# Four adaLN gate chunks of the second layer moved into its attention, and RMS and LayerNorm roots as one GpSimd power

## The chip, the cores and the metric

The kernel runs on one core of one Trainium2 chip. The metric is the device time of one execution in microseconds (us). TensorE (PE), VectorE (DVE), ScalarE (ACT), GpSimd (POOL) and SyncE (SP) work beside one another, each with its own queue of instructions; SP and POOL also issue DMAs from theirs.

## The reference, cut to what matters

Two layers work on 640 tokens (128 of context, 512 latent, D = 1024). The gate that the change moves is the last third of `mod`; the roots that it rewrites are those of `rms_norm(x, norm_g)` and of the convolution's `layer_norm`.

```
def trunk_layer(x, cond, p, latent, k_ctx, v_ctx):
    mod = silu(cond) @ p['w_ada'] + p['b_ada']        # 1024 x 3072
    shift, scale, gate = split(mod, 3, axis=-1)
    h = rms_norm(x, p['norm_g']) * (1.0 + scale) + shift
    y, k, v = parallel_mixer(h, p, latent, k_ctx, v_ctx)
    return x + gate * y, k, v

def rms_norm(x, g):   y = x * rsqrt(mean(x * x, -1) + EPS);  return y * g
def layer_norm(x, g, b):
    xc = x - mean(x, -1)
    return xc * rsqrt(mean(xc * xc, -1) + EPS) * g + b
```

`parallel_mixer` projects h by `w_in` (1024 x 11264) and runs four branches on it: a convolution module with that LayerNorm, a Hyena long convolution, a pooling mixer, and attention. Their gated outputs go through `wo_*`, are merged, and go through `w_out`. The gate is used only where the layer's output is added to x, so the second layer's gate is needed at its very end.

## The kernel before, in words

Every large matrix product is done in three products of halves: a weight tile of 512 KB is split into `whi` and `wlo`, the activations into a high and a low part (both called `sl` in the trace). `weights()` takes one of three pairs of whi/wlo buffers (the ring `wr`), SP loads the tile into one of two `raw` buffers, ACT casts it to `whi` and writes minus `whi` into `wlo`, and POOL issues a DMA that adds the tile to `wlo` in place (line 347). PE then multiplies 16 instructions with `whi` and 8 with `wlo` for each half of 320 tokens.

The adaLN product is cut into twelve chunks of 256 columns for each layer. `ada_chunk(l, j)` takes one slot of the same ring `wr`, but without a cast: SP loads the two halves of a chunk straight into the `whi` and `wlo` buffer (line 658), PE multiplies eight instructions of 32x256, which the trace shows as 16 records (`ax<-whi,cs` and `ax<-wlo,cs`, eight of each), and ACT copies the result to a tile `k`. Chunks 8 to 11 are the gate: SP stores `k` to DRAM as `grow` (line 672), and `gate_rows(l)` reads it back near the layer's end. `ada_later(jobs, step, start)` runs a list of chunks as a background thread: it waits `start` us of the planner's clock, and `step` us behind each chunk.

The order of work is made by a planner in Python, the class `Loom`: each stage is a thread with a priority (a smaller number goes first), and the planner, with its own modelled clocks, writes PE's order by hand. The other engines take their instructions in an order that follows from it, and SP and POOL issue their DMAs in that order. So a thread that is spawned elsewhere also changes the planner's later choices.

The first layer's four gate chunks and eight of the second layer's chunks run as a thread of priority 5 in the first layer's attention, one every `ASTEP` = 14 us. The second layer's four gate chunks run between the layers: they are spawned when the first layer's `out_proj` begins, with start `GS` = 40 us, no step and priority 50. At the same place `modulated(1, ...)` makes the second layer's h, in two groups of 128-token tiles (three, then two): `rms()` sums the squares and takes the root on DVE (`rmsv`, then `rmsr`), PE transposes it to a row (`ax<-ident,rmsr`), ACT copies the row (`t<-ax`), and for each of eight k DVE multiplies (`u<-sl,t`) and ACT and DVE write the two halves of h (`sl<-u,mod` and `sl<-u,mod,sl`). Behind it PE begins the second layer's `w_in`.

`rsqrt()` makes a root of 11 small DVE instructions: a first guess by two integer operations, and three Newton steps of three. `power()` is one `tensor_tensor` of POOL with the operation pow; before the change only the Hyena filters use it (`frs<-fv,nhalf`). `Conv.norm` takes the LayerNorm's root in each layer (`lnv`, then `lnr`), and PE spreads it by transposes (`sc<-ident,lnr`).

Of the kernel before, what the change touches and what calls it, by code (L numbers as in the profile page):

```python
# [21 lines left out]
DEPTH = 2  # L22
# [12 lines left out]
HW = 80  # L35
HA = 40
PL = 1
GS = 40.0
EACH = 0.003
ORD = "01456237vkq"  # L40
WAHEAD = 120
# [6 lines left out]
ASTEP = 14.0  # L48
ASTART = 60.0
LATA = 1.2  # L50
# [182 lines left out]
def hybrid_flow_backbone(ctx: ExitStack, tc: tile.TileContext, i, o):  # L233
    nc = tc.nc
    lm = Loom()
# [23 lines left out]
    def nm(p):  # L259
        count[0] += 1  # L260
        return f"{p}{count[0]}"
# [52 lines left out]
    def split(hi, lo, src, scale=None):  # L314
        if scale is None:
            act.copy(hi, src)
            dve.tensor_tensor(out=lo, in0=src, in1=r32(hi), op=ALU.subtract)
        else:
            act.activation(out=hi, in_=src, func=AF.Copy, scale=scale)
            dve.scalar_tensor_tensor(out=lo, in0=src, scalar=scale, in1=r32(hi),  # L320
                                     op0=ALU.mult, op1=ALU.subtract)
# [59 lines left out]
    def new_act(n):  # L381
        hi = yield from slots(n, F32R)
        lo = yield from slots(n, F32R)
        return Act(hi, lo)
# [102 lines left out]
    def power(out, v, n):  # L487

        pool.tensor_tensor(out=out, in0=v, in1=nhalf.to_broadcast([P, n]), op=ALU.pow)

    def rsqrt(out, v, n):

        t = sm.tile([P, 40], F32, tag="rsq_t", name=nm("rt"))[:, 0:n]
        dve.tensor_scalar(out=out.bitcast(I32), in0=v.bitcast(I32), scalar1=1, scalar2=None,
                          op0=ALU.logical_shift_right)
        dve.tensor_scalar(out=out.bitcast(I32), in0=out.bitcast(I32), scalar1=-1.0,
                          scalar2=1597463007.0, op0=ALU.mult, op1=ALU.add)
        for _ in range(3):
            dve.tensor_tensor(out=t, in0=out, in1=out, op=ALU.mult)
            dve.scalar_tensor_tensor(out=t, in0=t, scalar=-0.5, in1=v, op0=ALU.mult, op1=ALU.mult)  # L500
            dve.scalar_tensor_tensor(out=out, in0=t, scalar=1.5, in1=out, op0=ALU.add, op1=ALU.mult)
# [38 lines left out]
    def par(l, ct, row):  # L540
        return prm[:, ct, pcol(l, row):pcol(l, row) + 1]
# [150 lines left out]
    def ada_finish(l, p):  # L692

        ng = prm[:, 2 * (p % 2):2 * (p % 2) + 2, pcol(l, R_NG) + p // 2]
        for cnd in range(2):
            v = mods[l][:, 1, 2 * p:2 * p + 2, cnd]
            dve.scalar_tensor_tensor(out=v, in0=v, scalar=1.0, in1=ng, op0=ALU.add, op1=ALU.mult)
        ev_mod[l][p].set()
# [10 lines left out]
    def ada_later(jobs, step, start):  # L709
        yield lm.pe + start  # L710
        for l, j in jobs:
            yield from ada_chunk(l, j)
            if 4 <= j < 8:
                ada_finish(l, j - 4)
            yield lm.pe + step
# [34 lines left out]
    def rms(ssq):  # L750
        n = ssq.shape[1]
        v = sm.tile([P, 5], F32, tag="rmsv", name=nm("rmsv"))[:, 0:n]
        rs = sm.tile([P, 5], F32, tag="rmsr", name=nm("rmsr"))[:, 0:n]
        dve.tensor_reduce(out=v, in_=ssq, axis=AX.X, op=ALU.add)
        dve.tensor_scalar(out=v, in0=v, scalar1=1.0 / D, scalar2=EPS, op0=ALU.mult, op1=ALU.add)
        rsqrt(rs, v, n)
        return rs

    def modulated_first(a, xs, ssq):
# [89 lines left out]
    def merge(l, b, ga, nk, wo, merged, mode, ma=None, wait=None):  # L849


        for d in range(8):
            if mode == "last" and d % 4 == 0:
                for part in (ma.hi, ma.lo):
                    part.append((yield from slot(F32R)))
            th = yield from tr.get(T)

            def gate(j, ps):
                act.activation(out=th[:, 320 * j:320 * j + 320], in_=ps, func=AF.Tanh, scale=0.5)

            yield from in_proj(l, C_GM + b * D + 128 * d, gate)
            if wait is not None:
                yield wait
            w = yield from weights(wo[:, 128 * d:128 * d + 128].rearrange("(k p) c -> p k c", p=P), nk, 128)
            def take(j, ps):
                tj = th[:, 320 * j:320 * j + 320]
                dve.scalar_tensor_tensor(out=tj, in0=tj, scalar=1.0, in1=ps, op0=ALU.add, op1=ALU.mult)

            yield from both(w, 0, ga, nk, take)
            wr.put(WD)  # L870
            if mode == "first":
                sp.dma_start(out=mscr[l, d], in_=th)
                lm.cur.t += 2.5
            else:
                yield lambda: 0.0 if len(merged) == 2 else INF
                mv = merged[d // 4].v((d % 4) * T, T)
                dve.tensor_tensor(out=mv, in0=mv, in1=th, op=ALU.add)
                if mode == "last":
                    split(ma.h(d), ma.l(d), mv, 0.5)
            tr.put()  # L880
# [735 lines left out]
    class Conv:  # L1616
# [58 lines left out]
        def norm(self):  # L1675

            l = self.l
            yield self.ev_tap
            co = self.co
            pm = yield from sc.get()  # L1680
            for j in range(2):
                pe.matmul(pm[:, j, 0:328], lnw.to_broadcast([P, P]), self.pad.v(328 * j, 328), start=True, stop=True)
            self.pad.free()
            for c in range(4):
                x = co.v(656 * c, 656)
                xh = x.rearrange("p (a b) -> p a b", a=2)
                yield turn
                dve.tensor_tensor(out=xh, in0=xh, in1=pm[:, :, 0:328], op=ALU.subtract)
            sc.put()
            for c in range(4):  # L1690
                sq = yield from ur.get(656)
                act.activation(out=sq, in_=co.v(656 * c, 656), func=AF.Square)
                if c == 0:
                    total = sq
                else:
                    dve.tensor_tensor(out=total, in0=total, in1=sq, op=ALU.add)
                    ur.put()
            yield lm.sync()
            pvv = yield from ax.get()
            for t in range(5):  # L1700
                t0 = 0 if t == 0 else 143 + 128 * (t - 1)
                pe.matmul(pvv[:, t:t + 1], total[:, t0:t0 + 128], lnw, start=True, stop=True)
            ur.put(0.0)
            v = sm.tile([P, 5], F32, tag="lnv", name=nm("lnv"))
            rs = sm.tile([P, 5], F32, tag="lnr", name=nm("lnr"))
            dve.tensor_scalar(out=v, in0=pvv[:, 0:5], scalar1=EPS, scalar2=None, op0=ALU.add)
            ax.put()
            rsqrt(rs, v, 5)
            yield lm.sync()
            pr = yield from sc.get()  # L1710
            for t in range(5):
                dst = pr[:, 1, 0:128] if t == 0 else pr[:, 0, 128 * (t - 1):128 * t]
                pe.transpose(dst, rs[:, t:t + 1].to_broadcast([P, P]), ident)
            self.sa = sa = yield from new_act(1)
            for c in range(4):
                x = co.v(656 * c, 656)
                xn = yield from ur.get(T)
                dve.tensor_tensor(out=xn[:, 0:128], in0=x[:, 0:128], in1=pr[:, 1, 0:128], op=ALU.mult)
                yield turn
                dve.tensor_tensor(out=xn[:, 128:640], in0=x[:, 143:655], in1=pr[:, 0, :], op=ALU.mult)  # L1720
                yield turn
                dve.tensor_scalar(out=xn, in0=xn, scalar1=par(l, c, R_LNG), scalar2=par(l, c, R_LNB),
                                  op0=ALU.mult, op1=ALU.add)
                th = yield from ur.get(T)
                act.activation(out=th, in_=xn, func=AF.Tanh, scale=0.5)
                yield turn
                dve.scalar_tensor_tensor(out=xn, in0=th, scalar=1.0, in1=xn, op0=ALU.add, op1=ALU.mult)
                ur.put()
                split(sa.h(c), sa.l(c), xn, 0.5)
                ur.put()  # L1730
            sc.put()
            co.free()
            self.ev_norm.set()
# [157 lines left out]
    def layers():  # L1891
# [3 lines left out]
        for l in range(DEPTH):  # L1895
# [37 lines left out]
            lm.spawn(at.values_out(), 0, LATV)  # L1933
            lm.spawn(at.run(), 5.5)
            lm.spawn(at.parts(), 4)
            yield hy.ev_done
            yield from merge(l, 1, hy.gb, 4, i["wo_hyena"][l], None, "first")
            hy.gb.free()
# [35 lines left out]
            else:  # L1974
                load_x(xs, scratch[0:LP], scratch[LP:T])
            ssq = sm.tile([P, 5, 4], F32, tag="ssq", name=nm("ssq"))
            if l + 1 < DEPTH:
                lm.spawn(ada_later([(1, j) for j in range(8, 12)], 0.0, GS), 50, LATA)
            if l + 1 < DEPTH:
                xT = yield from slots(2)  # L1980
                evs = [[Event(lm) for _ in range(2)] for _ in range(4)]
# [180 lines left out]
```

## Time and profile before

| | |
|---|---|
| three runs, us | 2267.57, 2272.85, 2273.87 (median 2272.85) |
| the profiled execution, us | 2271.39 |
| its span, us | 2269.6 |
| granted TensorE clock, mean of the span | 0.992 |
| PE busy | 2189.7 us (96%), 15951 instructions |
| DVE, ACT, POOL busy | 59%, 52%, 26% |

The span is what lies between the first and the last instruction of the trace; the time of the execution is 1.8 us more. A row of a timeline gives start and length in us, then the engine, the line, the operation, the names (written from read), the size of one, and how many follow one another; in brackets stands how long the engine was idle just before, and what it waited for. Windows give busy time of each engine in a stretch, and the granted clock as a share of full speed.

### The profile page before, as it was taken

The page shows a single profiled execution, that of the slowest core. Times are in us where ns is not written, and L with a number is a line of the kernel's source. Part 1 is how long each engine was busy: PE and PEld are TensorE (multiplying, and loading weights), DVE is VectorE, ACT ScalarE, POOL GpSimd, SP SyncE. Part 2 cuts the span into 40 slices and gives each one's busy share as a digit, 9 for nine tenths or more (in the row PEclk, how much of TensorE's full clock was granted, in tenths as well). Part 3 has the DMA queues.
Part 4 walks back from the last instruction along what each step waited for, and adds up shares of the span by engine and source line. Part 5 has one row for each costly group of instructions (what it writes and reads, how often), then busy time and mean ns, then how long its engine had stood idle before and what let it go on. Part 6 is the DMA issues. An engine that isn't in the chain of part 4 may idle for free. (4 is left out here: it accounts for less than half of the span.)

```text
span 2269.6 us, 40007 instructions
## 1 busy us (share of the span) xinstructions
PE 2189.7 (96%) x15951; PEld 2140.5 (94%) x15951; DVE 1329.2 (59%) x2791; ACT 1190.8 (52%) x2179; POOL 585.5 (26%) x451
## 2 busy tenths in 40 slices
PE   5999999999999999999997999999999999999999
PEld 3899999999999998999996999999999999999999
DVE  5676786656679945443224677855764899612222
ACT  5544457667664345444445544656676543544442
POOL 1744321111012222554211333111111122222221
PEclk9899999999999999999998999999999999999999
DMA  8476775545568879778898865555466698698986
GB/s 277 110 156 137 156 159 114 97 95 99 106 122 147 149 126 182 154 164 161 150 220 239 154 118 120 110 102 101 84 110 118 126 155 150 120 162 148 174 171 138
DMA packets 510536, 322.33 MB, mean 142 GB/s; under 512 B 13016, under 2 KB 499608, under 8 KB 510093
## 3 DMA queue, kind: packets, MB, share of 16 engines
q0 software_dynamic: 223856, 122.96, 42.7%
q1 hardware_dynamic: 285780, 196.68, 28.6%
q8 instruction: 125, 2.05, 0.4%
q14 instruction: 62, 0.51, 0.1%
q10 hardware_dynamic: 713, 0.14, 0.0%
HBM read 302.26 MB, written 17.47 MB: 141 GB/s over the span
## 5 line engine op out<-in xcount | busy, mean ns | idle before, releaser
L193 PE MATMUL mm<-sl,whi 128*128 128x320 f32 x6304 | 1059.1, 313 | 10.6 <-DVE t L178 3.2
L193 PEld LDWEIGHTS mm<-sl,whi 128*128 128x128 f32 x6304 | 951.2, 189 | 18.2 <-DVE sl L178 4.3
L193 PE MATMUL mm<-sl,wlo 128*128 128x320 f32 x3152 | 555.1, 312 | 5.7 <-DMA wlo<-in_w_in_dram 5.7
L347 POOL DMA_DIRECT2D wlo<-in_w_in_dram x173 | 264.4, 1532 | 915.6 <-ACT wlo L178 689.5
L193 PEld LDWEIGHTS mm<-sl,wlo 128*128 128x128 f32 x3152 | 484.0, 189 | 7.4 <-DMA wlo<-in_w_in_dram 6.7
L178 ACT CAST whi<-raw 128x1024 fp32r<-128x1024 f32 (+2 forms) x272 | 255.3, 939 | 429.4 <-PE mm L193 405.1
L178 ACT ACTIVATE wlo<-whi 128x1024 fp32r<-128x1024 f32 (+2 forms) x269 | 254.9, 948 | 29.6 <-PE mm L193 25.7
L178 DVE SCALAR_TENSOR_TENSOR t<-t,mm 128x320 f32<-128x320 f32 x192 | 93.0, 485 | 294.1 <-PE mm L193 244.4
L193 PE MATMUL mm<-whi,sl 128*128 128x256 f32 x1600 | 226.2, 284 | 2.5 <-ACT u L178 1.5
L178 DVE SCALAR_TENSOR_TENSOR sc<-sl,prm,sc 128x640 f32<-128x640 f32 (+14 forms) x232 | 207.3, 893 | 11.4 <-ACT sc L178 6.7
L193 PE MATMUL sc<-sl,sl 128*128 128x128 f32 (+1 forms) x1344 | 203.4, 293 | 5.7 <-DVE u L178 2.8
L193 PEld LDWEIGHTS mm<-whi,sl 128*128 128x128 f32 x1600 | 203.3, 188 | 4.8 <-ACT u L178 1.7
L178 DVE TENSOR_TENSOR h<-ax,h 128x512 fp32r<-128x512 f32 (+1 forms) x200 | 120.1, 604 | 118.7 <-ACT h L178 117.5
L193 PEld LDWEIGHTS sc<-sl,sl 128*128 128x128 f32 x1344 | 179.5, 194 | 8.0 <-DVE u L178 4.0
L178 ACT ACTIVATE t<-mm 128x320 f32<-128x320 f32 x208 | 90.0, 433 | 137.8 <-PE mm L193 135.1
L178 DVE TENSOR_SCALAR_CACHE_REDUCE u<-sc,rq 128x640 f32<-128x640 f32 x128 | 112.6, 880 | 46.2 <-PE sc L193 45.2
L178 ACT ACTIVATE u<-u,nb 128x640 f32<-128x640 f32 x128 | 106.2, 830 | 52.3 <-DVE u L178 51.6
L178 ACT CAST h<-ax 128x512 fp32r<-128x512 f32 (+1 forms) x200 | 102.5, 515 | 55.8 <-PE ax L202 53.6
L193 PE MATMUL mm<-wlo,sl 128*128 128x256 f32 x800 | 126.7, 281 | 4.4 <-DMA wlo<-in_w_in_dram 4.4
L193 PE MATMUL ax<-h,sl 128*128 128x256 f32 (+1 forms) x656 | 120.7, 295 | 4.0 <-DVE h L178 2.7
L202 PE MATMUL ax<-ident,u 128*128 128x128 f32 x752 | 118.5, 273 | 4.7 <-DVE h L178 2.6
L193 PEld LDWEIGHTS mm<-wlo,sl 128*128 128x128 f32 x800 | 108.3, 188 | 5.0 <-DMA wlo<-in_w_in_dram 5.0
(211 smaller groups left out, 2225.9 us busy)
## 6 DMA issues: line engine op xcount, KB each, us to landing
raw<-in_w_in_dram SPq DMA_DIRECT2D x176, 512.0 KB
wlo<-in_w_in_dram POOLq DMA_DIRECT2D x173, 512.0 KB, 6.6
wlo<-in_w_ada_dram SPq DMA_DIRECT2D x19, 512.0 KB
whi<-in_w_ada_dram SPq DMA_DIRECT2D x19, 512.0 KB
raw<-in_wo_attn_dram SPq DMA_DIRECT2D x16, 512.0 KB
wlo<-in_wo_attn_dram POOLq DMA_DIRECT2D x16, 512.0 KB, 6.4
raw<-in_w_out_dram SPq DMA_DIRECT2D x16, 512.0 KB
wlo<-in_w_out_dram POOLq DMA_DIRECT2D x16, 512.0 KB, 6.0
```

The source lines that it names most:

```text
L178: r = f(*args, **kw)
L193: r = self.real.matmul(out, lhsT, rhs, **kw)
L202: r = self.real.transpose(out, in_, ident)
L347: nc.gpsimd.dma_start(out=lo[:, 0:w].rearrange("p (k c) -> p k c", k=kk), in_=src.bitcast(F32R), accum_op=ALU.add)
```

## The change

Two things change. The four gate chunks of the second layer are no longer spawned between the layers but behind the second layer's `at.parts()`, with step 14 us and priority 5. And `rms()` (three calls: 128x5 at the start, 128x3 and 128x2 between the layers) and `Conv.norm` (128x5 in each layer) call `power()` instead of `rsqrt()`. The roots of the attention's head norms stay on DVE.

```
@@ -35,7 +35,6 @@
-GS = 40.0
@@ -753,7 +752,7 @@            (rms)
         dve.tensor_scalar(out=v, in0=v, scalar1=1.0 / D, scalar2=EPS, op0=ALU.mult, op1=ALU.add)
-        rsqrt(rs, v, n)
+        power(rs, v, n)
         return rs
@@ -1705,7 +1704,7 @@          (Conv.norm)
             ax.put()
-            rsqrt(rs, v, 5)
+            power(rs, v, 5)
             yield lm.sync()
@@ -1933,6 +1932,8 @@          (the layers' main thread)
             lm.spawn(at.parts(), 4)
+            if l:
+                lm.spawn(ada_later([(1, j) for j in range(8, 12)], ASTEP, 0.0), 5, LATA)
             yield hy.ev_done
@@ -1974,8 +1975,6 @@
             ssq = sm.tile([P, 5, 4], F32, tag="ssq", name=nm("ssq"))
-            if l + 1 < DEPTH:
-                lm.spawn(ada_later([(1, j) for j in range(8, 12)], 0.0, GS), 50, LATA)
             if l + 1 < DEPTH:
```

Line numbers after the change are smaller by one, since one constant is gone. On PE, between the layers, the rows before were these. `ax<-whi,cs` and `ax<-wlo,cs` are gate chunks, `<-ident,sl` are transposes of x, and the last rows are the first tile of the second layer's `w_in`.

```order
L202 MATMUL ax_13003<-ident,sl_12254 128x128
L193 MATMUL ax_13010<-whi_13006,cs 32x256 x4
L193 MATMUL ax_13010<-wlo_13008,cs 32x256 x4
L202 MATMUL mm_13025<-ident,sl_12254 128x128 x2
L202 MATMUL ax_13032<-ident,sl_12254 128x128
L202 MATMUL mm_13045<-ident,sl_12254 128x128 x2
L202 MATMUL ax_13049<-ident,sl_12254 128x128
L193 MATMUL ax_13052<-whi_13035,cs 32x256 x4
L193 MATMUL ax_13052<-wlo_13037,cs 32x256 x4
```

The same place after the change, up to the first row of `w_in`:

```order
L201 MATMUL ax_12970<-ident,sl_12232 128x128
L201 MATMUL mm_12979<-ident,sl_12232 128x128 x2
L201 MATMUL ax_12983<-ident,sl_12232 128x128
L201 MATMUL mm_12992<-ident,sl_12232 128x128 x2
L201 MATMUL ax_12996<-ident,sl_12232 128x128
L201 MATMUL mm_13011<-ident,sl_12232 128x128 x2
L201 MATMUL mm_13015<-ident,sl_12232 128x128 x2
L192 MATMUL mm_13057<-sl_12240,whi_13044 128x320
```

The chunks are gone from between the transposes, and the transposes stand directly ahead of the first tile. A chunk is two rows of four instructions here, and there were four of them.

On SP's queue the rows before held eight chunk loads and, further on, four stores of `grow` between the first two `raw` loads of the second layer's `w_in` and the third. `xscratch` is a store of x, `spec` a load for the Hyena filters.

```order
L342 DMA raw_13159<-in_w_in_dram 128x8x128
L342 DMA raw_13169<-in_w_in_dram 128x8x128
L658 DMA whi_13006<-in_w_ada_dram 128x4x256
L729 DMA xscratch<-sl_12254 128x256
L730 DMA xscratch<-sl_12254 128x4x256
L658 DMA wlo_13008<-in_w_ada_dram 128x4x256
L325 DMA sl_13145<-spec 128x1280
L729 DMA xscratch<-sl_12254 128x256
L325 DMA sl_13145<-spec 128x1280
L658 DMA whi_13035<-in_w_ada_dram 128x4x256
```

After the change the same stretch of SP's queue, from the same two loads on, reads:

```order
L341 DMA raw_13043<-in_w_in_dram 128x8x128
L341 DMA raw_13050<-in_w_in_dram 128x8x128
L729 DMA xscratch<-sl_12232 128x4x256
L728 DMA xscratch<-sl_12232 128x256
L324 DMA sl_13029<-spec 128x1280 x2
L728 DMA xscratch<-sl_12232 128x256
L341 DMA raw_13220<-in_w_in_dram 128x8x128
L341 DMA raw_13287<-in_w_in_dram 128x8x128
```

The third and fourth loads of `w_in` follow with only stores of x and filter loads ahead of them.

In the second layer, where the chunks now stand on PE, the first of them reads so (it lies between two tiles of the projection of the values, keys and queries):

```order
L192 MATMUL mm_15044<-whi_15077,sl_12243 128x256 x4
L192 MATMUL mm_15044<-wlo_15078,sl_12241 128x256 x4
L192 MATMUL ax_15179<-whi_15175,cs 32x256 x4
L192 MATMUL ax_15179<-wlo_15177,cs 32x256 x4
L192 MATMUL mm_15202<-whi_15196,sl_12240 128x256 x4
```

The other three follow within some 300 rows of PE's order, and on SP's queue their loads stand between loads of `w_in` and `wo_hyena`. On POOL five powers are new; those between the layers stand next to the `wlo` additions of `w_in`:

```order
L346 DMA wlo_13045<-in_w_in_dram 128x8x128
L177 TENSOR_TENSOR rmsr_12909<-rmsv_12908,nhalf 128x3
L346 DMA wlo_13052<-in_w_in_dram 128x8x128
L177 TENSOR_TENSOR rmsr_13069<-rmsv_13068,nhalf 128x2
L346 DMA wlo_13222<-in_w_in_dram 128x8x128
```

Before, the three additions stood there with nothing between them, and each power now waits behind the addition ahead of it.

## Rows read from the trace of the kernel before

**Rows 1.** The page: busy time, share of the span and instructions of each engine.
```profile
PE 2189.7 (96%) x15951; PEld 2140.5 (94%) x15951; DVE 1329.2 (59%) x2791; ACT 1190.8 (52%) x2179; POOL 585.5 (26%) x451
```

**Rows 2.** Busy time and granted clock between the layers, and at the LayerNorm.
```profile
1200.00:1250.00 50.00, 37.82 (x252) 31.54 (x252) 24.21 (x84) 28.97 (x66) 6.24 (x4) 0.86 0.86 216
...
856.00:862.00 6.00, 5.09 (x26) 5.12 (x27) 4.68 (x12) 1.18 (x2) 0.00 (x0) 0.72 1.24 231
```

**Rows 3.** What PE waited for between 1200 and 1250 us (total, times, longest).
```profile
PE mm L193 <- DMA wlo<-in_w_in_dram: 4.9, 2, 2.6
PE ax L193 <- DMA wlo<-in_w_ada_dram: 3.8, 3, 2.3
...
PE ax L193 <- DMA whi<-in_w_ada_dram: 1.3, 2, 0.9
```

**Rows 4.** Timeline of DVE between the layers.
```profile
1203.55 0.17 DVE L178 TENSOR_SCALAR rmsv<-rmsv 128x3 f32<-128x3 f32 x1
...
1205.73 0.16 DVE L178 SCALAR_TENSOR_TENSOR rmsr<-rt,rmsr 128x3 f32<-128x3 f32 x1
...
1220.91 0.49 DVE L178 TENSOR_TENSOR u<-sl,t 128x320 f32<-128x320 f32 x1 [2.78 <-ACT sl L178]
```

**Rows 5.** Timeline of ACT between the layers.
```profile
1214.93 0.37 ACT L178 COPY k<-ax 128x256 f32<-128x256 f32 x1 [2.25 <-PE ax L193]
...
1216.10 1.98 ACT L178 CAST whi<-raw 128x1024 fp32r<-128x1024 f32 x2
1217.98 2.00 ACT L178 ACTIVATE wlo<-whi 128x1024 fp32r<-128x1024 f32 x2
...
1223.30 1.12 ACT L178 ACTIVATE sl<-u,mod 128x192 fp32r<-128x192 f32 x3
```

**Rows 6.** Timeline of PE between the layers.
```profile
1221.04 4.30 PE L193 MATMUL mm<-sl,whi 128*128 128x320 f32 x16
1227.92 1.44 PE L193 MATMUL mm<-sl,wlo 128*128 128x320 f32 x4 [2.58 <-DMA wlo<-in_w_in_dram]
...
1246.99 1.33 PE L193 MATMUL mm<-sl,wlo 128*128 128x320 f32 x8
1248.16 1.04 PE L193 MATMUL mm<-sl,whi 128*128 128x320 f32 x6
```

**Rows 7.** PE in the first layer's attention: one chunk at full clock.
```profile
154.11 0.64 PE L193 MATMUL ax<-whi,cs 128*32 128x256 f32 x8
154.57 0.61 PE L193 MATMUL ax<-wlo,cs 128*32 128x256 f32 x8
```

**Rows 8.** PE's waits for weights: between 100 and 400 us, then 1400 and 1800.
```profile
PE mm L193 <- DMA wlo<-in_w_in_dram: 1.5, 2, 1.2
PE mm L193 <- DMA wlo<-in_w_in_dram: 2.9, 1, 2.9
```

**Rows 9.** PE around the first layer's LayerNorm.
```profile
851.64 2.59 PE L193 MATMUL mm<-sl,whi 128*128 128x320 f32 x16
...
856.91 0.73 PE L202 MATMUL sc<-ident,lnr 128*128 128x128 f32 x5 [2.08 <-DVE lnr L178]
...
858.15 3.97 PE L193 MATMUL mm<-sl,whi 128*128 128x320 f32 x16
```

**Rows 10.** DVE around the first layer's LayerNorm.
```profile
851.82 0.17 DVE L178 TENSOR_SCALAR lnv<-ax 128x5 f32<-128x5 f32 x1 [0.31 <-PE ax L193]
851.90 0.81 DVE L178 TENSOR_TENSOR sl<-sl,t 128x640 f32<-128x640 f32 x1
...
855.21 0.68 DVE L178 TENSOR_TENSOR sl<-sl,sl 128x512 fp32r<-128x512 f32 x1
```

**Rows 11.** The powers of the Hyena filters: ns min/median/max, first and last start.
```profile
L178 POOL TENSOR_TENSOR frs<-fv,nhalf x16: 701/1030/1528, 68.0 to 1046.2; 128x2 f32<-128x2 f32 x16
```

**Rows 12.** PE at the second layer's LayerNorm, and in the start.
```profile
1958.68 0.71 PE L202 MATMUL sc<-ident,lnr 128*128 128x128 f32 x5
...
45.60 0.64 PE L193 MATMUL ax<-sl,cs 128*32 128x256 f32 x8 [1.13 <-DMA sl<-in_w_ada_dram]
```

More of the change, by code (lines that the diff above doesn't have):

```diff
@@ L37 @@
 PL = 1
-GS = 40.0
 EACH = 0.003
@@ L755, in rms @@
         dve.tensor_scalar(out=v, in0=v, scalar1=1.0 / D, scalar2=EPS, op0=ALU.mult, op1=ALU.add)
-        rsqrt(rs, v, n)
+        power(rs, v, n)
         return rs
@@ L1707, in norm @@
             ax.put()
-            rsqrt(rs, v, 5)
+            power(rs, v, 5)
             yield lm.sync()
@@ L1935, in layers @@
             lm.spawn(at.parts(), 4)
+            if l:
+                lm.spawn(ada_later([(1, j) for j in range(8, 12)], ASTEP, 0.0), 5, LATA)
             yield hy.ev_done
@@ L1976, in layers @@
             ssq = sm.tile([P, 5, 4], F32, tag="ssq", name=nm("ssq"))
-            if l + 1 < DEPTH:
-                lm.spawn(ada_later([(1, j) for j in range(8, 12)], 0.0, GS), 50, LATA)
             if l + 1 < DEPTH:
```

## The prediction, made before the changed kernel ran

> **What bounds the kernel now.** I read the busy times first: PE works 2189.7 of 2269.6 us [rows 1], so the kernel is bound by TensorE and only 79.9 us are idle. An edit on another engine is worth what it takes from PE's idle time or adds to PE's work. I therefore went to the windows for the stretches with the most idle time near the edits. Between the layers, in 1200 to 1250 us, PE is busy for 37.82 of 50 us, and the granted clock is 0.86 [rows 2]: 12.2 us are idle, and about 50 x 0.14 = 7.0 us more go to the lower clock. PE's waits there name the loads of `w_in` and of the gate chunks [rows 3]. The timelines of the four engines tell what holds what, and the same views at the two LayerNorms tell whether PE waits for a root.
>
> The profiled execution took 2271.39 us, 1.46 below the median and inside the runs' own spread (2267.57 to 2273.87), so its timeline stands for the median. All sums are made against it.
>
> **Between the layers: what leaves.** I follow the stretch from the end of the mean square at 1203.72 to the second layer's third weight tile, which PE begins at 1248.16 [rows 4, 6]. After that row PE runs closely before, and should after.
>
> 1. The root. Newton ends at 1205.89 [rows 4]. One power takes 1.03 us, the median of 16 of the same form with two elements [rows 11], so it would end at about 1204.8: -1.1 (with 0.70 and 1.53 as the ends, -1.5 to -0.6; three elements instead of two are not in the trace, and I take them at the same price). Ahead of the power in POOL's queue stands an addition to `wlo` whose cast is made well before, so the power doesn't wait for it.
>
> 2. ACT, which with DVE makes h. Its last output of the first group ends at 1223.30 + 1.12 = 1224.42 [rows 5]. On the way it waits 2.25 us with a copy `k<-ax` at the head of its queue, for a chunk whose load is late; with the chunks gone this wait goes, and so do three such copies of 0.37. Two casts and two `wlo` of 1.98 and 2.00 stand in the middle [rows 5]; in the new order ACT's first cast for `w_in` has moved ahead of the boundary, since no chunk holds a ring slot, and one pair stays: -2.0. Together 2.25 + 1.1 + 2.0 = 5.35. DVE waits 2.78 for ACT in this stretch [rows 4], so it follows ACT.
>
> 3. PE's first tile of `w_in` begins at 1221.04, as the last chunk ends; it would be paced by h instead, which is ready 6.4 us earlier by steps 1 and 2. Its 16 instructions take 4.30 [rows 6] where the same 16 take 2.59 elsewhere [rows 9], at the lower clock that follows PE's waits. I give back these 1.7.
>
> 4. PE waits 4.9 us in two places for `wlo` of `w_in` [rows 3], as ACT finished both `wlo` only at 1219.98 [rows 5] and the additions could begin only then. With the loads ahead in SP's queue and the first cast ahead of the boundary, both should have landed: -4.9.
>
> The sum is -1.1 - 5.35 - 1.7 - 4.9 = -13. PE's waits for chunk loads (3.8 + 1.3) [rows 3] are not counted again: they lie inside steps 2 and 3. What is late next is the chain of ACT and DVE through eight k. The nearer end is -6.2: only the waits for chunk loads and 1.1 of the root go, and the rest is held by ACT, DVE or the same DMAs. The farther end is -19.2: all 12.2 idle and all 7.0 of clock. I take -13 since each of its terms has its own row.
>
> **In the second layer's attention: what arrives.** PE is full there, so each chunk costs its own length. At full clock this is from 154.11 to 154.57 + 0.61, 1.07 us [rows 7] (one of ten between 99 and 278 us): 4 x 1.07 = +4.3. A chunk also holds one of three ring slots, and SP's two loads for it wait in SP's queue until the slot is free; every `raw` load behind them waits too, and for those ACT's cast, POOL's addition and then PE. The first layer ran its chunks in the same way with the same step, and PE waited only 1.5 us for `wlo` between 100 and 400 us [rows 8], nothing of it for chunk loads. So the lower end is 0; the upper is one wait of 2.9 us, the longest of this kind between 1400 and 1800 [rows 8], for each chunk: 11.6. I take +1, near the row of the first layer. ACT's copies (0.37) and the stores of `grow` fall on engines with room, and the gate is read only at the layer's end.
>
> **The LayerNorms.** In the first layer PE waits 2.08 us for the root, until 856.91, so it had come there at 854.83 [rows 9]. The variance is ready at 851.99 [rows 10]; a power of 1.03 ends at about 853.0, with 1.53 at 853.5, and PE would not wait. Behind the wait 16 instructions take 3.97 against 2.59 just ahead of it [rows 9], at a granted clock of 0.72 [rows 2], so up to 1.4 more could come back; I take half: -2.8 in all, between 0 and -3.5. The power delays the addition to `wlo` behind it on POOL by at most its own length, which three weight buffers cover; uncovered it would cost 1 us. In the second layer PE goes from the product before to the transposes with no wait [rows 12]: 0.
>
> **The start and the rest.** The first RMS root ends near 32 us, but PE waits there for loads, as still at 45.60 [rows 12]: 0. The planner also moves other instructions, in the first layer's filters and in both attentions. I put this at 0, with 3 us to either side (an estimate: a twentieth of the some 65 us of idle time outside the places above).
>
> Sum: -13 + 4.3 + 1 - 2.8 = -10.5, and 2271.4 - 10.5 = 2261.
>
> **The rivals.**
>
> A. The boundary is held by ACT and DVE anyway. Eight k pass through both, and PE's first two tiles need all of them. Then it gives 6.2, the attention takes 4.3 + 1, and the LayerNorm half of its share, 1.4: 2271.4 - 6.2 + 5.3 - 1.4 = 2269, no change. For it: DVE and ACT are busy between the layers with nothing but this. Against it: ACT's own wait and casts stand in the middle of its queue [rows 5].
>
> B. Slower: chunks starve the weights. If each chunk makes PE wait as for the late tile, the attention takes 4 x (1.07 + 2.9) = 15.9; with A's boundary and LayerNorm this is 2271.4 + 15.9 - 7.6 = 2280. It is slower than before as soon as the chunks take more than the boundary and LayerNorm give: with -7.6 from 0.8 us of wait for each, with my -15.8 from 2.9. For it: each chunk takes a slot of three and stands on SP's queue ahead of `raw` loads. Against it: the first layer's ten chunks [rows 7, 8].
>
> C. The LayerNorm's power is held up. From 851.90 DVE runs a row of instructions that read two operands from SBUF [rows 10], and they close up when the Newton steps between them go: until about 851.99 + 3.9 (the seven such instructions from 851.90 to 855.89 without the Newton steps) DVE has no gap. If the power began only then it would end near 856.9, as late as the root before: -2.8 is lost, and the time is 2264. The powers of the filters, at most 1.53 long [rows 11], speak against a delay of that size. The Trainium skill, "SBUF — State Buffer", "Who interferes with whom", speaks for it: a VectorE instruction with two SBUF inputs and a GpSimd instruction that reads SBUF share a read port, and the one that comes later is blocked for the other's whole length. The spread from 0.70 to 1.53 in the row can be such blocking, by one instruction and not by a row of seven.
>
> D. The boundary gives its whole 19.2 and the LayerNorm 3.5: 2271.4 - 19.2 + 4.3 - 3.5 = 2253.
>
> **How the numbers follow.** The forecast, 2254 to 2268, has 0.57; A 0.20, B 0.08, C 0.10, D 0.05. A measurement of this kernel can tell about 0.3%, so faster is below 2266.0 and slower above 2279.7. Faster: 0.55 of the forecast, 0.08 of C and 0.05 of D, 0.68. Slower: B, 0.08. The same: A with what is left of the forecast and of C, 0.24. The range runs from just below D to above A: 2252 to 2271; B and little else lies outside.
>
> **What would show it.** Between the layers no chunk rows, the first `w_in` cast ahead of 1200, the third tile near 1235, and PE busy for more than 44 of the 50 us from 1200. In the second layer four pairs of chunk rows of some 1.07, no wait for their loads, and waits for `wlo` of at most 4 us between 1400 and 1800. At the first LayerNorm no wait for the root, which POOL ends ahead of 854. I am wrong if the third tile comes behind 1242, if PE's waits for weights in the attention grow by more than 4 us, or if waits at places that the change doesn't touch move by more than 3.

## The result, and the profile after

The changed kernel took 2259.7 us (median of four runs, 2257.91 to 2260.89) against 2271.95 for the kernel before beside it: a ratio of 0.9946, with a 95% interval of 0.9932 to 0.9961. In two later groups of runs, with five rounds each, the same pair gave 0.9928 (0.9916 to 0.9940) and 0.9930 (0.9918 to 0.9941). So the change is worth 12 to 16 us; the forecast was 10.5, to 2261. The profiled execution has a span of 2258.9 us, 10.7 less than before.

To see where the time went I cut each span at four places of TensorE that every version has in the same order: (A) from the start to the first `ax<-lnw,u`, where the first LayerNorm begins; (B) from there to the eight `mm<-whi,sl` of the first layer that stand just ahead of the transposes of the boundary's first root (at 1203.40 before); (C) from there to the fourth `wlo` group of the second layer's first weight tiles; (D) from there to the second layer's first `ax<-lnw,u`; (E) the rest. All are differences of starts in the timelines, in us:

| version | A | B | C | D | E |
|---|---|---|---|---|---|
| before | 850.6 | 352.8 | 43.6 | 707.9 | 314.7 |
| the change, first trace | 854.8 | 346.9 | 27.4 | 716.8 | 313.0 |
| the change, in the two later groups | 853.3, 851.3 | 347.1, 347.4 | 27.4, 27.5 | 716.4, 715.2 | 312.6, 314.4 |
| chunks moved, roots Newton | 848.1 | 354.9 | 29.2 | 713.5 | 313.3 |
| powers alone | 854.5 | 347.0 | 39.7 | 712.4 | 312.1 |
| change, Newton at the start (two traces) | 850.7, 850.0 | 350.3, 348.0 | 28.1, 27.5 | 713.1, 712.8 | 311.0, 312.2 |
| change, Newton in the LayerNorms | 854.9 | 351.6 | 27.7 | 713.8 | 316.2 |
| change, Newton between the layers | 850.7 | 350.4 | 29.1 | 715.3 | 312.3 |
| change, no gate chunks (two traces) | 851.8, 853.5 | 346.6, 346.2 | 27.9, 27.4 | 711.3, 709.8 | 314.8, 314.3 |
| chunks behind the attention, Newton at the start | 848.3 | 355.0 | 27.5 | 714.8 | 316.9 |
| power at the start alone | 854.5 | 354.9 | 41.5 | 715.8 | 318.0 |

The rows of one version differ by up to 3.5 in A and about 2 in B, D and E from trace to trace; C repeats within 0.7. So C is read from one trace, and the others are read from several, or from the timed runs. The profiled execution of the chunks behind the attention took 2264.23 us, 9.7 above that version's median, so its row is read for C alone. D and E are best read as a sum: before, without gate chunks, and with the chunks behind the attention, 18 instructions of 128x320 stand behind the second layer's `ax<-lnw,u`, and in all other versions ahead of it. That moves some 2.6 us from E to D (an estimate: 16 such instructions take 2.35 from start to start).

Between the layers the windows and TensorE's waits, which answer to [rows 2, 3], are now these (start:end, length, then busy time of PE, PEld, DVE, ACT and POOL, granted clock, DMA share, GB/s):

```profile
1200.00:1250.00 50.00, 45.54 (x302) 42.50 (x301) 27.27 (x78) 36.45 (x77) 10.79 (x8) 0.97 0.87 184
```

```profile
PE mm L201 <- ACT sl L177: 2.2, 3, 0.8
PE mm L192 <- ACT sl L177: 1.4, 2, 0.8
PE ax L201 <- POOL rmsr L177: 0.3, 1, 0.3
```

TensorE is busy for 45.54 of 50 us instead of 37.82, and no wait for a load is left: it waits for what ACT makes, 0.8 us at most. The timeline of TensorE, which answers to [rows 6], shows the same place 18 us earlier:

```profile
1203.02 0.54 PE L201 MATMUL ax<-ident,rmsr 128*128 128x128 f32 x3 [0.26 <-POOL rmsr L177]
...
1212.11 4.40 PE L192 MATMUL mm<-sl,whi 128*128 128x320 f32 x16 [0.81 <-ACT sl L177]
1216.35 0.74 PE L192 MATMUL mm<-sl,wlo 128*128 128x320 f32 x4
1216.93 0.38 PE L201 MATMUL ax<-ident,rmsr 128*128 128x128 f32 x2
1217.07 0.84 PE L192 MATMUL mm<-sl,wlo 128*128 128x320 f32 x4
1217.74 2.50 PE L192 MATMUL mm<-sl,whi 128*128 128x320 f32 x16
1220.08 1.33 PE L192 MATMUL mm<-sl,wlo 128*128 128x320 f32 x8
...
1229.06 1.33 PE L192 MATMUL mm<-sl,wlo 128*128 128x320 f32 x8
1230.23 2.50 PE L192 MATMUL mm<-sl,whi 128*128 128x320 f32 x16
```

Before, the second tile read so:

```profile
1230.65 3.75 PE L193 MATMUL mm<-sl,whi 128*128 128x320 f32 x16
1236.69 2.41 PE L193 MATMUL mm<-sl,wlo 128*128 128x320 f32 x8 [2.29 <-DMA wlo<-in_w_in_dram]
```

The `wlo` groups now follow their tile at once, where they waited 2.58 and 2.29 before, and the second tile runs at full pace: the granted clock is 1.00 in 1216.35 to 1221.25, and was 0.66 in 1227.9 to 1238.9 before. The third tile begins at 1230.23. The reason for the waits stands on POOL. Before, ACT finished both `wlo` only at 1219.98 [rows 5], and both additions stand in one row:

```profile
1219.46 3.14 POOL L347 DMA_DIRECT2D wlo<-in_w_in_dram  x2 [33.09 <-ACT wlo L178]
```

Now they are apart:

```profile
1194.29 1.56 POOL L346 DMA_DIRECT2D wlo<-in_w_in_dram  x1 [9.52 <-ACT o L177]
1202.09 0.88 POOL L177 TENSOR_TENSOR rmsr<-rmsv,nhalf 128x3 f32<-128x3 f32 x1 [6.24 <-DVE rmsv L177]
1206.67 1.60 POOL L346 DMA_DIRECT2D wlo<-in_w_in_dram  x1 [3.71 <-ACT wlo L177]
1209.48 0.72 POOL L177 TENSOR_TENSOR rmsr<-rmsv,nhalf 128x2 f32<-128x2 f32 x1 [1.21 <-DVE rmsv L177]
```

The first addition starts 25 us earlier and the second about 14, and the two powers fit between.

At the first LayerNorm (before: [rows 9, 10]) TensorE reaches the transposes of the root with no wait, and the 16 instructions behind them run at full pace:

```profile
858.27 0.75 PE L192 MATMUL mm<-sl,wlo 128*128 128x320 f32 x4
858.87 0.71 PE L201 MATMUL sc<-ident,lnr 128*128 128x128 f32 x5
...
860.00 2.52 PE L192 MATMUL mm<-sl,whi 128*128 128x320 f32 x16
```

In the second layer's attention a chunk has the length that it had in the first layer (1.07 us, [rows 7]). In the waits of 1390 to 1790 us none is for a chunk's loads or for `wlo`; the two longest are for ACT:

```profile
1411.74 0.64 PE L192 MATMUL ax<-whi,cs 128*32 128x256 f32 x8
1412.20 0.61 PE L192 MATMUL ax<-wlo,cs 128*32 128x256 f32 x8
...
1418.61 0.55 PE L201 MATMUL ax<-ident,k 128*128 128x128 f32 x3 [3.63 <-ACT k L177]
```

```profile
PE ax L201 <- ACT k L177: 3.6, 1, 3.6
PE ax L201 <- ACT u L177: 2.4, 1, 2.4
```

### The profile page after: what moved, and what is told of

It reads as the page before. It is cut to its first block, busy times and chain, and to the rows that moved or that the text cites. A ratio compares the mean times of both kernels' runs of the same rounds, so it can differ in the third digit from the quotient of the medians.

```text
span 2258.9 us, 39947 instructions
## 1 busy us (share of the span) xinstructions
PE 2191.6 (97%) x15951; PEld 2141.9 (95%) x15951; DVE 1320.8 (58%) x2736; ACT 1191.5 (53%) x2179; POOL 593.5 (26%) x456
## 5 line engine op out<-in xcount | busy, mean ns | idle before, releaser
L177 DVE TENSOR_SCALAR_CACHE_REDUCE u<-sc,rq 128x640 f32<-128x640 f32 x128 | 112.7, 881 | 43.8 <-PE sc L192 42.6
```

The costliest lines, as they stand in the source:

```text
L177: r = f(*args, **kw)
```

## The experiments

The times are medians; a ratio is to the kernel before in the same group of runs, with its 95% interval. The kernels of a group ran on one chip, and there are three groups of four.

**Chunks moved, all roots Newton** (first group). All edits are to the changed kernel unless it is said otherwise.

```
-        power(rs, v, n)
+        rsqrt(rs, v, n)
...
-            power(rs, v, 5)
+            rsqrt(rs, v, 5)
```

> The chunks are moved as in the change, but all five roots stay Newton steps on VectorE. I cut the span at four places of TensorE: the first row ax<-lnw,u (first LayerNorm), the last rows mm<-whi,sl of the first layer, the fourth wlo group of the second layer's first weight tiles, the second layer's first ax<-lnw,u. Before: 850.6, 352.8, 43.6, 707.9 and 314.7 us to the end; after the change: 854.8, 346.9, 27.4, 716.8, 313.0. Theory 1 (each stretch belongs to the part of the change that stands in it, and the start's power re-lays the first layer's order): 850.6, 352.8, about 29 (the root is 1.3 us later than with the power), 716 to 717, 313 to 315: 2265 to 2267. Rival (the boundary's gain comes mostly from the roots, which free ACT and VectorE): the boundary stays at 36 or more, and the time near 2270.

2262.12 us, ratio 0.9954 (0.9940 to 0.9967). C is 29.2: moving the chunks alone takes 14.4 of the 16.2 us out of the boundary. The first theory holds in C and misses the total by 3 to 5, of which 3 stand in D.

**Powers alone** (first group). This is the kernel before with the roots changed and the chunks left where they were.

```
-        rsqrt(rs, v, n)
+        power(rs, v, n)
...
-            rsqrt(rs, v, 5)
+            power(rs, v, 5)
```

> The five roots are powers as in the change, but the four gate chunks stay between the layers. Same five stretches. Theory 1: 854.8, 346.9, 42.5 (the root comes 1.3 us earlier and little else), 707.9, 313 to 315: 2267 (in all -4 to -5: the LayerNorm's 5.9 and 1.3 gained, 4.2 lost in the first layer's filters). Rival (the roots make the boundary's gain): boundary 36 or less, 2260.

2268.44 us, ratio 0.9975 (0.9965 to 0.9985). C is 39.7, so with the chunks still there the earlier root is worth 3.9, more than the 1.1 expected, but the waits for loads stay:

```profile
PE mm L193 <- DMA wlo<-in_w_in_dram: 4.9, 2, 3.0
PE ax L193 <- DMA wlo<-in_w_ada_dram: 1.8, 3, 1.3
```

The rival (the roots make the boundary's gain) falls.

**The change with Newton at the start** (first and third group).

```
-        power(rs, v, n)
+        (rsqrt if n == 5 else power)(rs, v, n)
```

> The whole change, but the first root, 128x5 at the start, stays Newton steps; by the order of instructions TensorE's first layer is then as before, up to the boundary. Theory 1 (the start's power costs 4.2 us, through the planner's new order in the first layer): the first stretch is 850.6 again and the time 2255 to 2256. Rival (the 4.2 us come from the powers of the filters that meet other work on GpSimd, or from one run to another): the first stretch stays at 853 to 855 and the time at 2260.

2254.86 us, ratio 0.9918 (0.9906 to 0.9929), with A at 850.7. The first theory's numbers came, but the whole change was not in this group. So it was run again beside it:

> The whole change with the start's root on Newton steps once more, now beside the whole change on one chip. Theory 1: no wait for wlo near 439 us, and 3 to 5 us below the whole change. Rival (what the first group showed was the difference between two chips): within 1.5 us of it.

2253.33 us, ratio 0.9907 (0.9893 to 0.9922), against 2259.35 of the whole change (0.9930, 0.9918 to 0.9941): 6 us less by the medians, 5 by the ratios. This version is faster than both kernels.

**The power at the start alone** (third group). This is the kernel before with only its 128x5 root at the start a power.

```
-        rsqrt(rs, v, n)
+        (power if n == 5 else rsqrt)(rs, v, n)
```

> The kernel before with one root changed: only the first, 128x5 at the start, is a power. The traces so far show a wait of 2.9 to 3.4 us for wlo of w_in near 439 us in all six kernels with this power, and none there in the four without it. Theory 1 (this power alone re-lays the first layer's order and costs that wait, and nothing is won at the start): that wait is there, the first stretch is 852 to 855, and the time is 2 to 5 us above before. Rival (the start's power makes the first product begin earlier, so that both cancel): within 1 us of before.

2282.31 us, ratio 1.0033 (1.0022 to 1.0044): 7.4 us slower than before, more than the 2 to 5 expected. The wait is there. This is TensorE in this kernel:

```profile
433.79 0.75 PE L193 MATMUL mm<-whi,sl 128*128 128x256 f32 x5
437.55 1.22 PE L193 MATMUL mm<-wlo,sl 128*128 128x256 f32 x4 [3.00 <-DMA wlo<-in_w_in_dram]
```

and this in the whole change:

```profile
434.82 1.19 PE L192 MATMUL mm<-whi,sl 128*128 128x256 f32 x8
439.08 0.74 PE L192 MATMUL mm<-wlo,sl 128*128 128x256 f32 x4 [3.07 <-DMA wlo<-in_w_in_dram]
```

In the change with Newton at the start, between 390 and 460 us TensorE waits once, and not for a load:

```profile
PE ax L192 <- DVE sl L177: 1.0, 1, 1.0
```

All traces with the power at the start, nine with this one, have the wait (2.9 to 3.4 us); the five others, before among them, have none. In the whole change the tile is cast at 434.41 and its addition begins only at 437.32, while its first product is done at 436. The wait is shown, but it is not what the power at the start costs. Behind it TensorE waits less: from 445 us to the first LayerNorm it idles 2.8 us in this kernel and 6.3 before. In the whole of A it idles 41.5 to 43.7 us in the nine traces with this power and 41.1 to 43.8 in the five without, and A itself is 850.7 in a trace that has the power (Newton between the layers). In this kernel's trace (its execution took 2286.49) the idle time of the whole span is 83.7 us against 79.9 before, and the span is 15 longer; the rest lies in instructions that take longer, at a granted clock of 0.983 against 0.992.

The other order reaches into the second layer's attention as well. With Newton at the start TensorE idles 9.1 and 9.2 us in D, and 11.0 in the three traces of the whole change, whose wait of 2.4 for ACT's `u` is 0.2 there. It is 9.0 too with Newton in the LayerNorms, where the start is a power, so this order does not hang on the start's root alone.

**The change without gate chunks** (first and third group). The second layer's gate is read from the first layer's, so its own is not computed.

```
-            if l:
-                lm.spawn(ada_later([(1, j) for j in range(8, 12)], ASTEP, 0.0), 5, LATA)
...
-            yield ev_gate[l][n]
+            yield ev_gate[0][n]
-            load(r[n][0:2], grow[l, n][0:2])
+            load(r[n][0:2], grow[0, n][0:2])
...
-            load(r[n][3:P], grow[l, n][3:P])
+            load(r[n][3:P], grow[0, n][3:P])
```

> The whole change, but the second layer's four gate chunks are left out and its gate is read from the first layer's: 32 matrix products, eight loads of 256 KB x 2 and four stores less. Theory 1 (the chunks cost the second layer's attention 8.9 us, twice what was forecast): that stretch is 708 again, the other four as after the change, and the time 2251. Rival (the chunks cost their own 4.3 us, and the rest is another order of the attention or another clock): the stretch is 712 to 713, and the time 2255.

2253.22 us, ratio 0.9905 (0.9892 to 0.9918). D is 711.3, not 708. Again beside the whole change:

> The whole change with the second layer's gate chunks left out and its gate read from the first layer's, now beside the whole change on one chip. Theory 1 (a chunk costs its own 1.07 us and little more, some of it lying in idle time of the attention): 3 to 6 us below the whole change. Rival (the chunks starve the weights, 9 us): 8 to 10 below it.

2253.42 us, ratio 0.9912 (0.9899 to 0.9926): 5.9 below the whole change by the medians, 4 by the ratios, and D is 709.8 against 715.2, of which some 2.6 are the 18 instructions that stand in E here. The four chunks cost 4 to 6 us, their own 4.3 and little more. Without them the waits in 1390 to 1790 us begin so:

```profile
PE mm L192 <- DMA wlo<-in_w_in_dram: 3.1, 1, 3.1
PE ax L201 <- DVE h L177: 2.4, 3, 1.7
PE ax L201 <- ACT k L177: 2.1, 1, 2.1
```

A wait for `wlo` of 3.1 is there, as before, and is gone with the chunks; the wait for ACT's `k` is 2.1 instead of 3.6. A chunk replaces one wait by another; it does not starve the weights. D is still 2 to 3 us longer than before, with the same number of instructions, and TensorE idles as long in it (11.9 and 12.0 against 12.1). So these 2 to 3 us are no wait; what makes the instructions take longer is open.

**The whole change again** (second and third group, no edit), as the measure for the others:

> The whole change once more, beside the three others of this group, so that they are compared on one chip. If the first stretch (to the first LayerNorm) was 4.2 us longer through the order that the start's power makes, it is 852 to 855 again; if that was chance, it may be 849 to 851. The time: 0.9946 of before, within 0.002.

> The whole change, as the measure for the three others of this group: 0.993 to 0.995 of before.

2258.78 us (0.9928) and 2259.35 us (0.9930). A was 853.3 and 851.3, the second a miss for the expectation of the first: a part of the 4.2 was chance.

**Newton in the LayerNorms** (second group).

```
-            power(rs, v, 5)
+            rsqrt(rs, v, 5)
```

> The whole change, but the two LayerNorm roots are Newton steps on VectorE; order of TensorE's first layer as after the change. Theory 1 (the power takes away not only the 2.1 us wait for the root but what follows it: the wait of 1.6 for t at the next tile and the low clock): idle time of 850 to 900 us is 4.5 to 5 instead of 1.2, the clock there 0.93 to 0.97, and the time 4 to 6 us above the whole change. Rival (only the wait of 2.1 counts, the rest is made up later): 1.5 to 3 us above it.

2264.95 us, ratio 0.9953 (0.9941 to 0.9966), 6.2 above the whole change by the medians. B is 4.5 longer. TensorE's waits in 858 to 885 us are these:

```profile
861.17 0.73 PE L201 MATMUL sc<-ident,lnr 128*128 128x128 f32 x5 [2.08 <-DVE lnr L177]
867.20 2.60 PE L192 MATMUL mm<-sl,whi 128*128 128x320 f32 x16 [0.30 <-DVE t L177]
878.53 2.62 PE L192 MATMUL mm<-sl,whi 128*128 128x320 f32 x16 [2.79 <-DVE t L177]
```

The wait for the root is 2.08, as before. A second one of 2.79 comes 17 us later, for `t` of VectorE; with the power it is 0.30. The first theory holds: the Newton steps also make VectorE late, and TensorE pays again when it needs VectorE next. The 6.2 is more than the change gained, though. In this version TensorE waits 2.1 for the second layer's root as well, and E is 316.2 against 312.6; in the kernel before, in another order, there was no such wait [rows 12].

**Newton between the layers** (second group).

```
-        power(rs, v, n)
+        (power if n == 5 else rsqrt)(rs, v, n)
```

> The whole change, but the two roots between the layers are Newton steps; TensorE's order is the same as after the change, row by row. Theory 1 (the root stands on the path there and nothing else changes): the stretch from the first layer's last mm<-whi,sl to the fourth wlo group is 28.7 to 29.5 instead of 27.4, TensorE waits 1.4 for the root instead of 0.3, and the time is 1 to 2 us above the whole change. Rival (VectorE's 22 small instructions also slow the chain that makes h): 4 us above it.

2259.80 us, ratio 0.9936 (0.9921 to 0.9952), 1.0 above the whole change, which the intervals can't tell apart; the trace can: C is 29.1 against 27.4, and TensorE waits 1.5 for the root instead of 0.3. The two roots are worth 1.7 there.

**Chunks behind the attention** (second group). The start's root is Newton too, as above.

```
             lm.spawn(at.parts(), 4)
-            if l:
-                lm.spawn(ada_later([(1, j) for j in range(8, 12)], ASTEP, 0.0), 5, LATA)
...
             po.at = at
+            if l:
+                lm.spawn(ada_later([(1, j) for j in range(8, 12)], ASTEP, 0.0), 5, LATA)
```

> Start's root on Newton as in the third run, and the four chunks go behind the second layer's attention, into the last merge, where TensorE is busy all the time. Theory 1 (the attention has idle time into which a chunk partly fits, the last merge has none): the chunks cost their whole 4.3 us here, and the time is 0 to 2 us above that of the third run (0.9918 of before), so 0.992 to 0.993. Rival (in the attention the chunks starve the weights and cost 9): it is 3 to 5 us below it, 0.990.

2254.56 us, ratio 0.9917 (0.9902 to 0.9933), as the change with Newton at the start (0.9918 and 0.9907). In the trace the four chunks do not stand in the last merge but in the one behind the attention, at 1828 to 1880 us, and there TensorE is full (busy for 244.6 of the 245 us from 1700). They cost about the same there as in the attention. The rival (they starve the weights in the attention) falls; the first theory's 0 to 2 us are too small to tell.

## Why the prediction was right, and where it was not

**Between the layers: right in mechanism, 3 us too small.** Forecast -13, measured -16.2 (C), and the runs split it into 14.4 for the chunks and 1.8 for the roots, which the Newton run repeats at 1.7.

1. The root: -1.1 forecast. It ends 0.97 us behind the mean square instead of 2.17, so -1.2.
2. ACT's last output of the first group now ends at 1214.18 + 1.41 = 1215.59, 13.6 us behind the mean square at 1202.00 instead of 20.7 behind 1203.72: -7.1 with the root, where -6.5 was forecast.
3. The clock at the first tile was not given back: the 16 instructions take 4.40 instead of 4.30, at a granted clock of 0.62 in 1212 to 1216. Nor does h decide when the tile begins, as I had it: TensorE's waits for ACT ahead of it, the last one of 0.81 too, each end as ACT has copied transposes of x out of TensorE's output. The last of these copies ends at 1212.06, and the tile begins at 1212.11:

```profile
1211.59 0.47 ACT L177 ACTIVATE sl<-mm,mod 128x256 f32<-128x256 f32 x1
```

4. Both waits for `wlo`, 4.9, are gone, as forecast.

The term that was mis-sized is the clock of step 3. It came back behind the first tile, and it gave more than 1.7. From the first tile's `wlo` to the end of the second tile the rows took 2.73, 3.75 and 2.20 before, the two waits left out, and take 1.39, 2.34 and 1.17 now: 3.8 less. With 7.2 up to the first tile, 4.9 of waits and 0.3 in the second group of tiles this makes the 16.2.

**The attention: right.** +5.3 forecast; the two groups without chunks give 4 to 6. The chunks' own length makes that; the 1 us of waits in my sum did not come. `wlo` and the chunks' loads made no wait, and a longer wait for ACT's copies stands against it: TensorE idles 11.0 us in D with the chunks and 11.9 and 12.0 without.

**The first LayerNorm: right in direction, mis-sized.** -2.8 forecast (0 to -3.5). B is 5.4 to 5.9 shorter than before in the three traces of the whole change, and 4.5 shorter than with the roots back on Newton. The step that failed is "behind the wait ... I take half": the clock came back whole (the 16 instructions take 2.52 instead of 3.97), and I did not count the next wait for `t`, which is VectorE being late by its Newton steps. Before and after it reads:

```profile
874.25 2.62 PE L193 MATMUL mm<-sl,whi 128*128 128x320 f32 x16 [1.57 <-DVE t L178]
```

```profile
873.37 2.60 PE L192 MATMUL mm<-sl,whi 128*128 128x320 f32 x16 [0.30 <-DVE t L177]
```

The root's wait of 2.08, 1.45 of clock and 1.27 of this wait make 4.8.

Rival C is answered by the power itself. In the whole change it is

```profile
L177 POOL TENSOR_TENSOR lnr<-lnv,nhalf x2: 1704/1704/1705, 856.3 to 1947.4; 128x5 f32<-128x5 f32 x2
```

long (ns min/median/max) in both layers, and 128x5 at the start, where VectorE had nothing to do, took 1204. So it took 0.5 us more, but was not held by a row of seven instructions, as rival C has it. It began at 856.26, with POOL idle for 5.81 us before, beside an instruction of VectorE with two SBUF inputs that runs from 856.09 to 856.91, and ended at 857.97; TensorE came at 858.87. The Trainium skill, "SBUF — State Buffer", "Who interferes with whom", lets a GpSimd instruction that reads SBUF be blocked by such an instruction for its length; the trace agrees with a delay by one instruction (0.50 us, where 0.65 were left of it), and the six that follow on VectorE from 856.82 added nothing. The other runs show that VectorE makes the difference. In the two traces without gate chunks and in the one with the chunks behind the attention VectorE is idle beside the second layer's power, and there it takes 1.20; the other 17 powers of the LayerNorms have the same instruction of VectorE beside them and take 1.70 or 1.71.

**The start and the rest: the step that failed.** I put the first root and the planner's new order at 0, with 3 to either side. The root at the start by itself costs 7.4 us in the kernel before and 5 to 6 in the changed one. Nothing at the start itself is slower: the first product of `w_in` begins at 53.0 to 53.4 in the three traces of the first result and group that have the power, and at 52.4 to 54.4 in the three that don't. The planner, whose clocks took another root, wrote another order. In it a weight tile comes late at 439 us, a wait of 3.07 where there was none; the prediction's last sign of being wrong allows 3. But the same order saves as much idle time elsewhere in A. By the end of B (A and B together) the whole change stands at 1198.7 to 1201.7, and with Newton at the start it stands at 1201.0 and 1197.9. What differs is D and E together: 1029.0 to 1029.8 against 1024.0 and 1025.0. About 2 of these 5 us are waits in the attention, and the rest is the same work taking longer. Over the whole span TensorE idles 67 to 68 us in all five of these traces, but is busy for 2187.3 to 2191.6 us with the power and for 2185.2 and 2183.4 without. So the loss is shown; that it comes through the order is argued, and what makes the instructions take longer stays open.

**The sum.** -13 + 5.3 - 2.8 + 0 was forecast; the runs give about -16, +5, -5 to -6 and +5 to +7. These add to some -10, where 12 to 16 was measured; parts tried alone change the order too, so they need not add up. That the sum came out near is in part luck: the loss through the new order and the larger gains at the boundary and the LayerNorm offset one another. Of the rivals A (2269) fell, since the boundary gave 16.2 and not 6.2; B fell in the runs without chunks; D has the boundary's gain between the forecast and its own 19.2.

## What to carry to other kernels

Background work that a bound engine shares with a boundary is worth moving where its loads take no buffer slot that the next stage waits for: here 64 short records, 16 for each chunk, held up the first weight tiles by 14 us and cost 5 elsewhere. When a small chain leaves an engine, look one consumer further than the wait it ends in: here the same lateness was paid twice. And where a planner orders the whole program, a local edit is also a new order everywhere: compare the order far from the edit, and try each part alone, since one part of a winning change can cost half of it.

## What the runs showed of the hardware that I had not expected

The five new powers of GpSimd grow with their few elements: 0.72 us for 128x2, 0.88 for 128x3, 1.20 for 128x5, when no instruction of VectorE runs as they begin, and 1.70 for 128x5 when one with two SBUF inputs does (all 17 such powers, against 1.20 in the other three of the LayerNorms). These are the rows of the whole change between the layers and at the start; the one at the LayerNorms is shown above:

```profile
L177 POOL TENSOR_TENSOR rmsr<-rmsv,nhalf x3: 716/881/1204, 29.1 to 1209.5; 128x5 f32<-128x5 f32 x1, 128x3 f32<-128x3 f32 x1, 128x2 f32<-128x2 f32 x1
```

From 128x2 to 128x5 each further column of elements adds about 0.16 us, (1.204 - 0.716) / 3.

Form and VectorE are not all of it: a filter's power of 128x2 took 1.40 at 942.15, with no instruction of VectorE beside it but begun while POOL still issued an addition to `wlo` (941.19 to 942.79).
